# Down projection of the last two token groups: products in eight PSUM banks, raw weights in pieces of 128x512, output DMAs of the group before on another queue

## The chip, the cores and the metric

One Trainium2 chip, of which the kernel uses one core. The metric is the device time of one execution in microseconds; the time given is the median of the runs. The engines are TensorE (PE), VectorE (DVE), ScalarE (ACT), GpSimd (POOL) and SyncE (SP), each with an instruction queue of its own that it works off in order; DMAs are issued from such a queue too.

## What is computed

One layer of a streaming encoder in float32, on 2048 frames of width 1024 with 16 meta tokens ahead of them: RWKV-7 heads and forgetting-attention heads on a common input projection, a common output projection (`w_o`), and a gated MLP with a causal convolution (the Conv-FFN). The change touches the last part alone:

```python
h = x @ w_in                          # 1024 -> 2 x 2816
hp = pad(h, CONV_W - 1 ahead)         # CONV_W = 3
y = conv_b + sum(conv_w[i] * hp[:, i : i + L] for i in range(CONV_W))
u, gt = split(y, 2)
x = x + (silu(gt) * u) @ w_out        # 2816 -> 1024
```

## The kernel before, in words

Every float32 operand of TensorE is split into a high part and a low part in the type `F32R`: ScalarE casts the high part (`h`), VectorE or GpSimd subtracts it from the operand (`l`). A product is three matmuls per 128 of the contracted dimension: high by high, low by high, high by low. All matmuls of these products are issued by one helper, at L1121.

The Conv-FFN works on four groups of some 512 tokens, held with tokens along the free dimension. The hidden dimension is 22 blocks `f` of 128 (`FT`). The first two groups (`early`) go one by one through class `Ffn`: its `down` (L1226 on) multiplies the activated blocks by `w_out` and adds the products to `acc`, the group's residual stream (8 tiles `m` of 128 features by 512 tokens), and after the last block sends each tile to the output. The last two groups, `a` and `b`, go together through class `Last`, after `rest()` has finished the second early group and `w_o` has made their inputs `acca` and `accb`.

`Last` makes the up projection of both groups from seven products in place of eight, as Strassen and Winograd do it: sums of the weights' blocks (`raw` tiles, combined on GpSimd at L1342 to L1353: `s`, and three in place) meet sums of the inputs' blocks (`half_a`, `half_b`: `t1` to `t4`, `b2`, each with `h` and `l`; the `parts` helper is L1267 and L1268, `scaled` is L1273). `up(f)` is a generator for one block: it loads two raw weight tiles of 128x1024 (`ru`, `rg`, L1312), splits them (`qh`, `ql`, `rh`, `rl`: L1322, L1323, L1348, L1349), issues the products into four banks (`A`, `B`, `D`, `Cb`), copies and adds them into four tiles `c`, runs the convolution (`conv`: one ScalarE activation L1338 and two VectorE steps L1340 on a tile `v`), and the activation up to `zh`, `zl` (L1399 to L1405). `mlp` calls it for each `f`, and after every second block the `down` of the pair of blocks before. So there are eleven `down` calls. Each is 16 products of six matmuls: 8 tiles `m` by the groups `a` and `b`, each product in one PSUM bank, then added to `acca` or `accb` by VectorE (L1423). Its weights come in two halves of four `m`; a half is one raw tile of 128x1024, filled by two DMAs of 128x512 (L1414, one for each block of the pair) and split as a whole (L88 on ScalarE, L89 on VectorE).

PSUM has eight banks of 128x512: the pool `ffpA` hands out three (`bank`, name `pp`), the pool `ffpR` five (`bankR`, name `pr`). In the last stage the up projection uses `pr` and the down projection `pp`. SBUF tiles come from pools that are stacked; where a new pool lies on memory of a closed one, its first writes wait for the last uses of what was there. `L0` and `L1` are the pools of the split inputs, `L0` lies first, then `ffV` (`raw`, `qh`/`ql`, `r`, `s1`), then `L1`; they lie where the early groups had `acc`, `xh`, `xl`. `late_ops` lists what goes to `L0`.

The order of instructions on each engine is not written out: the framework schedules the program beforehand against a timeline of its own, which also decides which buffer of a ring an instruction gets. So a change of a ring or a bank moves instructions.

Of the kernel before, what the change touches and what calls it, by code (L numbers as in the profile page):

```python
# [68 lines left out]
def pcol(K, name, i=0):  # L69
    o, w = PC[name]  # L70
    return K.pc[:, o + i : o + i + 1]
# [14 lines left out]
def split(eng, K, src, hi, lo):  # L86

    K.nc.scalar.copy(hi, src)  # L88
    eng.tensor_sub(lo, src, hi.bitcast(F32))  # L89
# [1008 lines left out]
class Ffn:  # L1098
# [128 lines left out]
    def down(self, G, fs, zs):  # L1227
        K, nc, acc = self.K, self.K.nc, G.acc
        w = [self.weight(K.fout[f]) for f in fs]
        for m in range(KC):  # L1230
            ms = slice(128 * m, 128 * m + 128)
            for b, nb in G.blocks:
                p = G.out([128, 512])[:, :nb]
                self.product(p, [(wh[:, ms], wl[:, ms], zh[:, b : b + nb], zl[:, b : b + nb])
                                 for (wh, wl), (zh, zl) in zip(w, zs)])
                a = acc[:, m, b : b + nb]
                nc.vector.tensor_tensor(a, a, p, op=ALU.add)
            if fs[-1] == FT - 1:
                s = max(16 - G.T0, 0)
                nc.sync.dma_start(K.outT[m, :, G.T0 + s - 16 : G.T0 - 16 + G.n], acc[:, m, s : G.n])  # L1240

    def mlp(self, G, switch=FT, out=None):

# [12 lines left out]
class Last:  # L1256
# [51 lines left out]
    def up(self, f):  # L1308
        K, nc, W = self.K, self.K.nc, self.W
# [7 lines left out]
        bank = lambda: self.bank([128, 512])  # L1317
# [15 lines left out]
        vs = {}  # L1333

        def conv(i, j):
            t, k = c[i][j], f + i * FT
            v = vs[i, j] = self.C([128, 512], "v", 3)
            nc.scalar.activation(v, t[:, 2:], AF.Identity, bias=pcol(K, "cb", k), scale=pcol(K, "cw2", k))  # L1338
            for o in (1, 0):
                nc.vector.scalar_tensor_tensor(v, t[:, o : o + 512], pcol(K, f"cw{o}", k), v, op0=ALU.mult, op1=ALU.add)  # L1340
# [5 lines left out]
        for i, v in enumerate((au, ag)):  # L1346
            s = slice(256 * i, 256 * i + 256)
# [60 lines left out]
    def down(self, fs, zs):  # L1408
        K, nc = self.K, self.K.nc
        for m in range(KC):  # L1410
            if m % 4 == 0:
                raw, (h, l) = self.raw(), self.pair()
                for i, f in enumerate(fs):
                    nc.sync.dma_start(raw[:, 512 * i : 512 * i + 512], K.fout[f, :, 128 * m : 128 * m + 512])  # L1414
                split(nc.vector, K, raw, h, l)
                w = [(h[:, s : s + 512], l[:, s : s + 512]) for s in (0, 512)]
            ms = TILES[m % 4]
            for j, G in enumerate((self.a, self.b)):
                t = slice(512 * j, 512 * j + 512)
                p = self.out([128, 512])  # L1420
                self.F.product(p, [(wh[:, ms], wl[:, ms], zh[:, t], zl[:, t]) for (wh, wl), (zh, zl) in zip(w, zs)])
                a = G.acc[:, m]
                nc.vector.tensor_tensor(a, a, p, op=ALU.add)  # L1423
                if fs[-1] == FT - 1:
                    nc.sync.dma_start(K.outT[m, :, G.T0 - 16 : G.T0 - 16 + 512], a)
# [16 lines left out]
def tail(K, ctx, at, c0):  # L1442
# [6 lines left out]
    bank = lambda shape: pA(shape, "pp", 3)  # L1449
    turn = ExitStack()  # L1450
    with ExitStack() as c1:
# [16 lines left out]
        bankR = lambda shape: pR(shape, "pr", 5)  # L1468
# [13 lines left out]
        M = Last(F, a, b)  # L1482
# [2 lines left out]
        F.w_o(b)  # L1485
        rest()

    late_ops = ("t4h", "t4l", "t3h", "t3l", "b2h", "b2l", "rh", "rl")
    L0 = Pool(tc, late, "ffL0", side="left")
    M.W = Pool(tc, late, "ffV", side="left")  # L1490
    L = pools(L0, Pool(tc, late, "ffL1", side="left"), dict.fromkeys(late_ops, 0))
# [6 lines left out]
    turn.close()  # L1498
    M.C = Pool(tc, late, "ffC2", side="left")
    M.Z = Pool(tc, late, "ffZ", side="right")  # L1500
    M.bank, M.out = bankR, bank
    M.mlp()


# [50 lines left out]
```

## Time and profile before

| what | us |
|---|---|
| median of 3 runs | 3417.93 |
| the three runs | 3402.91, 3419.29, 3417.93 |
| the profiled execution | 3404.62 |
| span of the profiled execution | 3402.80 |
| TensorE busy | 3275.4 |
| VectorE busy | 2352.7 |
| ScalarE busy | 1664.9 |
| GpSimd busy | 1159.8 |

The times of the trace run from the span's start; 1.8 us of the profiled execution lie around the span. The last two groups' Conv-FFN takes the span from about 2662 us to the end. `[7.25 <-ACT qh L1322]` behind a row of a timeline means that the engine had idled 7.25 us just before, until ScalarE's instruction of that line had made `qh`. "x12" is the number of instructions that a row joins. The granted clock (PEclk) is a share of TensorE's full speed. An engine's busy time is counted in its instructions; issuing a DMA is not in it.

### The profile page before, as it was taken

To read this page: it belongs to the slowest core of one execution; us is meant where nothing else is said; L and a number is where in the kernel's file an instruction comes from. 1 tells how busy PE (TensorE), PEld (TensorE's weight loads), DVE (VectorE), ACT (ScalarE), POOL (GpSimd) and SP (SyncE) were. 2 spreads that over 40 slices of the span, in tenths; PEclk is the share of its full clock that TensorE was granted. 3 is DMA by queue.
4 is the path that set the end of the run, shared out by engine and by line. 5 is a ranking of instruction groups with operands and counts; after the bars stand their busy time and mean duration, and the time that the engine had idled before them with its cause. 6 is when DMAs were issued, how large, how long until landed. Compare 5 with 4: busy or idle time off the path is not lost.

```text
span 3402.8 us, 61891 instructions
## 1 busy us (share of the span) xinstructions
PE 3275.4 (96%) x23061; PEld 2906.4 (85%) x23061; DVE 2352.7 (69%) x4946; ACT 1664.9 (49%) x3529; POOL 1159.8 (34%) x1733
## 2 busy tenths in 40 slices
PE   7999999999999999999999999999999899999999
PEld 7889888988988988999999998888888677777777
DVE  5665666566556757887878886777665677667666
ACT  5542444554244457765666665654343343334342
POOL 4441112444111157755445453412014422222221
PEclk9999999999999999999999999999999899999999
DMA  4566333356634255333233344324233111111112
GB/s 111 122 133 154 105 93 102 99 121 133 158 88 108 78 172 162 116 107 111 80 89 100 94 130 132 94 73 158 94 98 115 65 50 50 41 53 56 38 50 87
DMA packets 346517, 341.93 MB, mean 100 GB/s; under 512 B 168376, under 2 KB 281256, under 8 KB 345192
## 3 DMA queue, kind: packets, MB, share of 16 engines
q1 hardware_dynamic: 346024, 337.91, 35.1%
q8 instruction: 182, 2.98, 0.4%
q14 instruction: 119, 0.97, 0.1%
q0 software_dynamic: 192, 0.07, 0.0%
HBM read 267.62 MB, written 70.27 MB: 99 GB/s over the span
## 4 chain that ended last, share of the span: by engine, by line
PE 48%; DVE 4%; DMA 3%; ACT 2%; issue 2%; POOL 2%; SPq 0%; ACTq 0%; POOLq 0%; DVEq 0%
PE pp L1121 23%; PE pr L1121 16%; PE o L1031 3%; PE pt L1011 3%; DMA raw<-d_qk 2%; PE s L961 1%; PE s L963 1%; DVE v L1340 1%; DVE rl L1349 1%; DMA raw<-in_fin_dram 1%; POOL kl L903 0%; ACT P L980 0%; ACT ph L1026 0%; DVE ql L89 0%; DVE c L1331 0%
## 5 line engine op out<-in xcount | busy, mean ns | idle before, releaser
L82 DVE TENSOR_TENSOR ww_lo<-ww_raw,ww_hi 128x1024 fp32r<-128x1024 f32 (+1 forms) x172 | 215.5, 1260 | 79.1 <-ACT ww_hi L81 45.0
L1121 PE MATMUL pp<-xh,ww_hi 128*128 128x256 f32 (+2 forms) x1248 | 248.3, 326 | 4.3 <-ACT xh L1186 3.2
L1121 PE MATMUL pp<-xh,ww_lo 128*128 128x256 f32 (+2 forms) x1248 | 250.3, 325 | 0.0
L1121 PE MATMUL pp<-xl,ww_hi 128*128 128x256 f32 (+2 forms) x1248 | 247.9, 324 | 0.0
L81 ACT CAST ww_hi<-ww_raw 128x1024 fp32r<-128x1024 f32 (+1 forms) x172 | 171.4, 1009 | 132.2 <-PE pp L1121 54.9
L1027 DVE TENSOR_TENSOR pl<-pt,ph 128x512 fp32r<-128x512 f32 (+2 forms) x352 | 196.2, 562 | 52.5 <-ACT ph L1026 50.8
L1026 ACT CAST ph<-pt 128x512 fp32r<-128x512 f32 (+2 forms) x352 | 167.6, 485 | 105.1 <-PE pt L1011 73.2
L954 DVE CUSTOM_DVE_ANT_0 P<-cb,s 16x16 f32<-16x16 f32 (+8 forms) x360 | 182.7, 519 | 51.6 <-PE s L963 28.5
L1121 PEld LDWEIGHTS pp<-xh,ww_hi 128*128 128x128 f32 x1248 | 191.2, 189 | 23.9 <-ACT xh L1186 4.5
L1121 PEld LDWEIGHTS pp<-xl,ww_hi 128*128 128x128 f32 x1248 | 194.0, 189 | 17.9
L1121 PEld LDWEIGHTS pp<-xh,ww_lo 128*128 128x128 f32 x1248 | 192.3, 189 | 16.9
L1011 PE MATMUL pt<-cst,P 128*128 128x128 f32 (+2 forms) x1224 | 202.1, 276 | 2.9 <-ACT P L980 1.6
L89 POOL TENSOR_TENSOR wi<-sq,kx 128x320 fp32r<-128x320 f32 (+2 forms) x48 | 48.6, 1012 | 397.7 <-ACT kx L88 296.1
L203 PE MATMUL pj<-xah,w_hi 128*128 128x384 f32 x480 | 166.0, 346 | 1.8 <-ACT xah L194 1.8
L1031 PE MATMUL o<-ph,vs 128*128 128x256 f32 x576 | 158.8, 285 | 6.7 <-ACT ph L1026 6.4
L205 PE MATMUL pj<-xah,w_lo 128*128 128x384 f32 x480 | 164.6, 343 | 0.4 <-DVE r L181 0.4
L204 PE MATMUL pj<-xal,w_hi 128*128 128x384 f32 x480 | 163.6, 341 | 0.0
L1340 DVE SCALAR_TENSOR_TENSOR v<-c,pc,v 128x512 f32<-128x512 f32 x176 | 145.0, 849 | 21.9 <-ACT v L1338 15.3
L1031 PE MATMUL o<-pl,vs 128*128 128x256 f32 x576 | 156.5, 290 | 2.9 <-DVE pl L1027 2.5
L980 ACT ACTIVATE P<-P,nm 128x656 f32<-128x656 f32 (+6 forms) x104 | 143.5, 1380 | 30.7 <-DVE nm L979 30.3
L203 PE MATMUL pj<-xbh,w_hi 128*128 128x320 f32 (+1 forms) x480 | 153.9, 321 | 0.0
L205 PE MATMUL pj<-xbh,w_lo 128*128 128x320 f32 (+1 forms) x480 | 153.8, 320 | 0.0
(501 smaller groups left out, 9859.2 us busy)
## 6 DMA issues: line engine op xcount, KB each, us to landing
ww_raw<-in_fin_dram SPq DMA_DIRECT2D x88, 512.0 KB, 3.6
w_raw<-in_wt_dram SPq DMA_DIRECT2D x60, 512.0 KB, 3.7
ww_raw<-in_fout_dram SPq DMA_DIRECT2D x44, 512.0 KB, 3.7
raw<-in_fin_dram SPq DMA_DIRECT2D x44, 512.0 KB, 3.7
xv<-d_var SPq DMA_DIRECT2D x32, 384.0 KB, 5.9
ww_raw<-in_wo_dram SPq DMA_DIRECT2D x24, 512.0 KB, 3.5
raw<-in_fout_dram SPq DMA_DIRECT2D x44, 256.0 KB, 2.9
raw<-d_qk SPq DMA_DIRECT2D x112, 88.0 KB, 2.6
```

The costliest lines, as they stand in the source:

```text
L81: nc.scalar.copy(hi, raw)
L82: nc.vector.tensor_sub(lo, raw, hi.bitcast(F32))
L203: nc.tensor.matmul(p, wh[:, c, :M], xh[:, c, :n], start=c == 0, stop=False)
L204: nc.tensor.matmul(p, wh[:, c, :M], xl[:, c, :n], start=False, stop=False)
L205: nc.tensor.matmul(p, wl[:, c, :M], xh[:, c, :n], start=False, stop=c == KC - 1)
L954: nc.vector.tensor_tensor_reduce(dst, c, src, 1.0, 3e38, op0=ALU.add, op1=ALU.min, accum_out=mx[:nq, np_ : np_ + 1])
L1011: nc.tensor.transpose(pt[:kn, x, c0 : c0 + nq], P[:nq, k0 : k0 + kn], K.ident[:nq, :nq])
L1026: nc.scalar.copy(ph[:kn, xs, c:N], pt[:kn, xs, c:N])
L1027: nc.vector.tensor_sub(pl[:kn, xs, c:N], pt[:kn, xs, c:N], ph[:kn, xs, c:N].bitcast(F32))
L1031: nc.tensor.matmul(o[:, c:N], vs[:kn, jj], pp[:kn, x, c:N], start=False, stop=jj == nt - 1 and y == 1)
L1121: self.K.nc.tensor.matmul(p, w, x, start=start and i == 0, stop=i == len(mms) - 1, skip_group_check=not start)
L1340: nc.vector.scalar_tensor_tensor(v, t[:, o : o + 512], pcol(K, f"cw{o}", k), v, op0=ALU.mult, op1=ALU.add)
```

## The change

Five edits. (1) In `Ffn.down` the output DMAs of the second early group are issued from GpSimd's queue and no longer from SyncE's. (2) The ring of `v` has two buffers in place of three. (3) In `Last.down` each piece of raw weights, 128x512 for one block of the pair, has a tile `rawd` of its own with one buffer, is loaded by one DMA and split by itself, in place of half a `raw` tile; the split results lie as before in two halves of `qh`, `ql`. (4) `t2l` goes to `L0`, which is then larger by 6 KB in each partition, and `ffV` begins that much further on: `raw` lies no longer on the memory of `acc` but on that of `xh`. (5) The banks for the products of `Last.down` come from `pp` and `pr` in turn; since groups `a` and `b` alternate, `a`'s products are in `pp` and `b`'s in `pr`, which the up projection keeps using.

```diff
--- before.py
+++ after.py
@@ -1,3 +1,4 @@
+import itertools
 import math
 from contextlib import ExitStack
 from types import SimpleNamespace
@@ -1237,7 +1238,8 @@
                 nc.vector.tensor_tensor(a, a, p, op=ALU.add)
             if fs[-1] == FT - 1:
                 s = max(16 - G.T0, 0)
-                nc.sync.dma_start(K.outT[m, :, G.T0 + s - 16 : G.T0 - 16 + G.n], acc[:, m, s : G.n])
+
+                (nc.gpsimd if G.last else nc.sync).dma_start(K.outT[m, :, G.T0 + s - 16 : G.T0 - 16 + G.n], acc[:, m, s : G.n])
 
     def mlp(self, G, switch=FT, out=None):
 
@@ -1334,7 +1336,7 @@
 
         def conv(i, j):
             t, k = c[i][j], f + i * FT
-            v = vs[i, j] = self.C([128, 512], "v", 3)
+            v = vs[i, j] = self.C([128, 512], "v", 2)
             nc.scalar.activation(v, t[:, 2:], AF.Identity, bias=pcol(K, "cb", k), scale=pcol(K, "cw2", k))
             for o in (1, 0):
                 nc.vector.scalar_tensor_tensor(v, t[:, o : o + 512], pcol(K, f"cw{o}", k), v, op0=ALU.mult, op1=ALU.add)
@@ -1409,11 +1411,12 @@
         K, nc = self.K, self.K.nc
         for m in range(KC):
             if m % 4 == 0:
-                raw, (h, l) = self.raw(), self.pair()
-                for i, f in enumerate(fs):
-                    nc.sync.dma_start(raw[:, 512 * i : 512 * i + 512], K.fout[f, :, 128 * m : 128 * m + 512])
-                split(nc.vector, K, raw, h, l)
+                h, l = self.pair()
                 w = [(h[:, s : s + 512], l[:, s : s + 512]) for s in (0, 512)]
+                for f, hl in zip(fs, w):
+                    raw = self.W([128, 512], "rawd")
+                    nc.sync.dma_start(raw, K.fout[f, :, 128 * m : 128 * m + 512])
+                    split(nc.vector, K, raw, *hl)
             ms = TILES[m % 4]
             for j, G in enumerate((self.a, self.b)):
                 t = slice(512 * j, 512 * j + 512)
@@ -1485,7 +1488,7 @@
         F.w_o(b)
         rest()
 
-    late_ops = ("t4h", "t4l", "t3h", "t3l", "b2h", "b2l", "rh", "rl")
+    late_ops = ("t4h", "t4l", "t3h", "t3l", "b2h", "b2l", "rh", "rl", "t2l")
     L0 = Pool(tc, late, "ffL0", side="left")
     M.W = Pool(tc, late, "ffV", side="left")
     L = pools(L0, Pool(tc, late, "ffL1", side="left"), dict.fromkeys(late_ops, 0))
@@ -1498,7 +1501,9 @@
     turn.close()
     M.C = Pool(tc, late, "ffC2", side="left")
     M.Z = Pool(tc, late, "ffZ", side="right")
-    M.bank, M.out = bankR, bank
+    M.bank = bankR
+    banks = itertools.cycle((bank, bankR))
+    M.out = lambda shape: next(banks)(shape)
     M.mlp()
 
 
```

Up to the last output DMAs of the second early group the order on all engines stays as it was; from there on it moves instructions, at these places above all. First GpSimd's queue at the end of `rest()`, where the stage of the last two groups begins (`r` and `E` make the scaling of the last group, `s` and the `raw` rows combine the first raw weights, `rl` is the low part of `rb`). Before:

```order
L1162 TENSOR_TENSOR ssum_32468<-ssum_32468,sqv_32687 128x512 [waits Activation_49]
L1162 TENSOR_TENSOR ssum_32468<-ssum_32468,sqv_32722 128x512 [waits Activation_49]
L1162 TENSOR_TENSOR ssum_32468<-ssum_32468,sqv_32757 128x512 [waits Activation_49]
L1173 TENSOR_TENSOR r_32765<-r_32765,mhalf_76 128x4 [waits DVE_49]
L100 TENSOR_SCALAR E_32769<-r_32765 128x512 [waits Pool_49]
L1342 TENSOR_TENSOR s_6058_32881<-raw_32878 128x384 [waits DMAHW5_49,PE_49]
L1351 TENSOR_TENSOR raw_32878<-raw_32877,raw_32878 128x384 [waits DMAHW3_49,DMAHW2_49,DMAHW4_49,DMAHW1_49,DMAHW6_49,DMAHW0_49,DMAHW7_49,DVE_49,Pool_49]
L1268 TENSOR_TENSOR rl_32938<-xs_6076_32934,rh_32937 128x1024 [waits Activation_49]
```

and now:

```order
L1163 TENSOR_TENSOR ssum_32468<-ssum_32468,sqv_32757 128x512 [waits Activation_49]
L1242 DMA out_dram<-acc_29102 128x512 [waits DVE_49] x5
L1174 TENSOR_TENSOR r_32765<-r_32765,mhalf_76 128x4 [waits DVE_49]
L101 TENSOR_SCALAR E_32769<-r_32765 128x512 [waits Pool_49]
L1242 DMA out_dram<-acc_29102 128x512 [waits DVE_49] x3
L1344 TENSOR_TENSOR s_6058_32881<-raw_32878 128x384 [waits DMAHW5_49,PE_49]
L1353 TENSOR_TENSOR raw_32878<-raw_32877,raw_32878 128x384 [waits DMAHW4_49,Pool_49]
L1354 TENSOR_TENSOR raw_32877<-s_6058_32881,raw_32877 128x384 [waits DVE_49,Pool_49]
L1270 TENSOR_TENSOR rl_32938<-xs_6076_32934,rh_32937 128x1024 [waits DMASW4_49,DMASW3_49,DMASW5_49,DMASW2_49,DMASW6_49,DMASW1_49,DMASW7_49,DMASW0_49,Activation_49]
```

The eight output DMAs stand among these instructions, five ahead of `r` and `E` and three ahead of `s`; `s` now waits for TensorE beside its own DMA.

Second TensorE's queue where a down projection begins, the third (`zh`, `zl` are the activated blocks of the pair, `rh` and `rl` with `pr` the end of the up projection). Before, from the last product of the up projection to the first product that needs a bank again:

```order
L1121 MATMUL pr_34272<-rh_32937,rh_34257 128x512 [waits Activation_49]
L1121 MATMUL pr_34272<-rh_32937,rh_34257 128x512
L1121 MATMUL pr_34272<-rl_32938,rh_34257 128x512 x2
L1121 MATMUL pr_34272<-rh_32937,rl_34258 128x512 x2
L1121 MATMUL pp_34400<-zh_34049,ql_34395 128x512 [waits DVE_49]
L1121 MATMUL pp_34400<-zh_34221,ql_34395 128x512
L1121 MATMUL pp_34408<-zh_34049,ql_34395 128x512
L1121 MATMUL pp_34408<-zh_34221,ql_34395 128x512
L1121 MATMUL pp_34416<-zh_34049,ql_34395 128x512
L1121 MATMUL pp_34416<-zh_34221,ql_34395 128x512
L1121 MATMUL pp_34424<-zh_34049,qh_34394 128x512 [waits DVE_49]
```

and now, from the first row of the down projection on:

```order
L1122 MATMUL pp_34415<-zh_34061,qh_34405 128x512 [waits Activation_49]
L1122 MATMUL pr_34423<-zh_34061,qh_34405 128x512
L1122 MATMUL pp_34431<-zh_34061,qh_34405 128x512
L1122 MATMUL pr_34439<-zh_34061,qh_34405 128x512
L1122 MATMUL pp_34447<-zh_34061,qh_34405 128x512
L1122 MATMUL pr_34284<-rh_32937,rh_34269 128x512 [waits Activation_49]
L1122 MATMUL pr_34284<-rh_32937,rh_34269 128x512
L1122 MATMUL pr_34284<-rl_32938,rh_34269 128x512 x2
L1122 MATMUL pr_34284<-rh_32937,rl_34270 128x512 x2
L1122 MATMUL pr_34455<-zh_34061,qh_34405 128x512 [waits DVE_49]
L1122 MATMUL pr_34471<-zh_34061,qh_34405 128x512 [waits DVE_49]
L1122 MATMUL pp_34415<-zh_34233,qh_34405 128x512 [waits Activation_49]
```

Before, the fourth product (`pp_34424`) waits for VectorE's addition of the first, behind 18 matmuls of three products and six of the up projection. Now the first five products get a bank at once, `pr_34455` and `pr_34471` take banks that the up projection's additions free, and the first row that waits for an addition of this down projection (`pp_34463`) stands 49 matmuls behind the first. The second half's rows that wait for the third and fourth piece of weights stand 48, 56 (casts) and 62, 67 (splits) matmuls behind it, that for the second piece's split 29.

Third VectorE's queue at the same place (`ql` from `raw` or `rawd` are the splits of the down projection's weights, `c` and `v` the convolution of the block, `rl` the next block's weights). Before:

```order
L89 TENSOR_TENSOR ql_34395<-raw_34393,qh_34394 128x1024 [waits DMAHW2_49,DMAHW3_49,PE_49,Activation_49]
L89 TENSOR_TENSOR ql_34466<-raw_34464,qh_34465 128x1024 [waits DMAHW4_49,DMAHW5_49,PE_49,Activation_49]
L1331 TENSOR_TENSOR c_6287_34268<-c_6287_34268,pr_34338 128x512 [waits Activation_49]
L1331 TENSOR_TENSOR c_6286_34267<-c_6286_34267,pr_34307 128x512 [waits PE_49]
L1340 SCALAR_TENSOR_TENSOR v_34537<-c_6287_34268,pc_70,v_34537 128x512 [waits Activation_49]
L1340 SCALAR_TENSOR_TENSOR v_34546<-c_6286_34267,pc_70,v_34546 128x512 [waits Activation_49]
L1340 SCALAR_TENSOR_TENSOR v_34537<-c_6287_34268,pc_70,v_34537 128x512 [waits DVE_49]
L1340 SCALAR_TENSOR_TENSOR v_34546<-c_6286_34267,pc_70,v_34546 128x512 [waits DVE_49]
L1331 TENSOR_TENSOR c_6288_34269<-c_6288_34269,pr_34272 128x512 [waits PE_49]
L1349 TENSOR_TENSOR rl_34572<-raw_34559,rh_34571 128x256 [waits DMAHW6_49,Activation_49]
L1349 TENSOR_TENSOR rl_34572<-raw_34560,rh_34571 128x256 [waits DMAHW7_49,Activation_49]
L1423 TENSOR_TENSOR acca_32134<-acca_32134,pp_34400 128x512 [waits PE_49]
```

and now:

```order
L90 TENSOR_TENSOR ql_34406<-rawd_34407,qh_34405 128x512 [waits DMAHW0_49,PE_49,Activation_49]
L1342 SCALAR_TENSOR_TENSOR v_34340<-c_6289_34278,pc_70,v_34340 128x512 [waits DVE_49]
L1333 TENSOR_TENSOR c_6291_34280<-c_6291_34280,pr_34350 128x512 [waits Activation_49]
L1333 TENSOR_TENSOR c_6290_34279<-c_6290_34279,pr_34319 128x512 [waits PE_49]
L1342 SCALAR_TENSOR_TENSOR v_34555<-c_6291_34280,pc_70,v_34555 128x512 [waits Activation_49]
L90 TENSOR_TENSOR ql_34406<-rawd_34411,qh_34405 128x512 [waits DMAHW5_49,Activation_49]
L1342 SCALAR_TENSOR_TENSOR v_34555<-c_6291_34280,pc_70,v_34555 128x512 [waits DVE_49]
L1333 TENSOR_TENSOR c_6292_34281<-c_6292_34281,pr_34284 128x512 [waits PE_49]
L1351 TENSOR_TENSOR rl_34590<-raw_34577,rh_34589 128x256 [waits DMAHW3_49,Activation_49]
L1351 TENSOR_TENSOR rl_34590<-raw_34578,rh_34589 128x256 [waits DMAHW4_49,Activation_49]
L1402 SCALAR_TENSOR_TENSOR v_34555<-c_6291_34280,v_34555 128x512 [waits Activation_49]
L90 TENSOR_TENSOR ql_34480<-rawd_34481,qh_34479 128x512 [waits DMAHW6_49,Activation_49]
```

The two splits of 1024 columns stood together ahead of additions and convolution steps. Now there are four of 512, one at a time between them; the fourth comes five rows behind the first additions to `acca` and `accb`, which begin two rows below the last row shown.

## Rows read from the trace of the kernel before

**Rows 1.** The page's first part: busy us, share of span, instructions.

```profile
PE 3275.4 (96%) x23061; PEld 2906.4 (85%) x23061; DVE 2352.7 (69%) x4946; ACT 1664.9 (49%) x3529; POOL 1159.8 (34%) x1733
```

**Rows 2.** Windows: busy us by engine, then PEclk, DMA share, GB/s.

```profile
2660.00:2700.00 40.00, 25.07 (x78) 18.22 (x77) 31.60 (x31) 14.85 (x21) 17.95 (x10) 0.74 0.21 73
...
3000.00:3200.00 200.00, 193.50 (x836) 156.32 (x835) 142.20 (x208) 79.16 (x136) 49.59 (x62) 1.00 0.16 50
```

**Rows 3.** What TensorE waited for in 2600:3403: us in total, times, longest us.

```profile
PE pp L1121 <- DVE acca L1423: 20.9, 10, 3.1
...
PE pr L1121 <- ACT t4h L1267: 3.4, 1, 3.4
```

**Rows 4.** TensorE's timeline, a down projection: start us, us, row, [idle before].

```profile
2875.78 0.63 PE L1121 MATMUL pp<-zh,qh 128*128 128x512 f32 x2
...
2879.96 1.56 PE L1121 MATMUL pp<-zh,ql 128*128 128x512 f32 x6
2883.85 0.73 PE L1121 MATMUL pp<-zh,qh 128*128 128x512 f32 x2 [2.32 <-DVE acca L1423]
```

**Rows 5.** VectorE's timeline around the same down projection.

```profile
2873.99 2.46 DVE L89 TENSOR_TENSOR ql<-raw,qh 128x1024 fp32r<-128x1024 f32 x2 [1.28 <-PE pr L1121]
...
2877.93 2.78 DVE L1340 SCALAR_TENSOR_TENSOR v<-c,pc,v 128x512 f32<-128x512 f32 x4 [0.29 <-ACT v L1338]
...
2883.12 0.67 DVE L1423 TENSOR_TENSOR acca<-acca,pp 128x512 f32<-128x512 f32 x1
```

**Rows 6.** Groups of instructions in 2700:3403: VectorE's splits and its 128x512 operations.

```profile
L1402 DVE SCALAR_TENSOR_TENSOR v<-v,v 128x512 f32<-128x512 f32 x44 | 30.0, 683 | 0.0
...
L89 DVE TENSOR_TENSOR ql<-raw,qh 128x1024 fp32r<-128x1024 f32 x22 | 26.3, 1224 | 14.6 <-PE pr L1121 12.2 <-ACT qh L88 2.4
```

**Rows 7.** SyncE's queue where the last two groups begin.

```profile
2651.72 10.93 SPq L1240 DMA_DIRECT2D out_dram<-acc  x8
2664.94 0.82 SPq L1312 DMA_DIRECT2D raw<-in_fin_dram  x2
```

**Rows 8.** TensorE's timeline where the last two groups begin.

```profile
2661.40 0.60 PE L103 MATMUL pp<-cst,E 128*128 128x128 f32 x4
2669.25 5.49 PE L1121 MATMUL pr<-p,qh 128*128 128x512 f32 x12 [7.25 <-ACT qh L1322]
...
2690.82 1.65 PE L1121 MATMUL pr<-t2h,qh 128*128 128x512 f32 x3 [0.75 <-ACT c L1361]
```

**Rows 9.** GpSimd's timeline where the last two groups begin.

```profile
2658.04 1.02 POOL L1173 TENSOR_TENSOR r<-r,mhalf 128x4 f32<-128x4 f32 x1 [5.63 <-DVE r L1172]
...
2670.04 6.67 POOL L1342 TENSOR_TENSOR s<-raw 128x384 f32<-128x384 f32 x1 [10.28 <-DMA raw<-in_fin_dram]
```

**Rows 10.** VectorE's timeline where the last two groups begin.

```profile
2656.55 0.69 DVE L1237 TENSOR_TENSOR acc<-acc,pr 128x512 f32<-128x512 f32 x1 [0.70 <-PE pr L1121]
...
2669.14 1.75 DVE L1268 TENSOR_TENSOR b2l<-b,b2h 128x1536 fp32r<-128x1536 f32 x1
2670.81 1.02 DVE L1323 TENSOR_TENSOR ql<-raw,qh 128x384 fp32r<-128x384 f32 x2
...
2677.29 0.92 DVE L1323 TENSOR_TENSOR ql<-s,qh 128x384 fp32r<-128x384 f32 x1 [1.46 <-ACT qh L1322]
2678.66 3.40 DVE L1268 TENSOR_TENSOR t1l<-xs,t1h 128x1536 fp32r<-128x1536 f32 x1 [0.46 <-ACT t1h L1267]
2681.99 2.55 DVE L1294 TENSOR_TENSOR xs<-xs,t 128x1536 f32<-128x1536 f32 x1
2684.46 2.29 DVE L1323 TENSOR_TENSOR ql<-raw,qh 128x384 fp32r<-128x384 f32 x3
```

**Rows 11.** DMA issues: KB each, median us from issue to landing.

```profile
raw<-in_fout_dram SPq DMA_DIRECT2D x44, 256.0 KB, 2.9
...
out_dram<-acc SPq DMA_DIRECT2D x16, 256.0 KB, 2.5
```

**Rows 12.** The DMAs that GpSimd issues before the change: ns min/median/max.

```profile
L282 POOL DMA_DIRECT2D d_fl<-st x6: 520/647/785, 49.9 to 671.1; - x6
```

## The prediction

> **What bounds the kernel now.** I read the page's first part, then the window table of the last stage, TensorE's waits in it, and the timelines of the engines that these waits name. TensorE is busy 96% of the span [rows 1], so a gain can only come from its idle time, or from fewer matmuls, and the change leaves their number as it is. In the Conv-FFN of the last two token groups one stretch of 200 us holds 193.5 us of matmuls, while VectorE, the next busiest, has 142 us of work in it [rows 2]: it is not a bound on the mean, but it may be late at a place. The list of waits says where: in ten of the eleven down projections a matmul waits for the first addition into `acca`, 20.9 us in all [rows 3]. The other large piece is the stretch in which the last two groups begin: 25.07 of 40 us busy, 14.9 us idle, at a mean granted clock of 0.74 [rows 2].
>
> In a down projection TensorE starts at 2875.78, fills the three `pp` banks with products, works them off to the low parts, and then needs a bank that VectorE has read; it idles 2.32 us and goes on at 2883.85 [rows 4]. VectorE comes late because it has two splits of 1024 columns (2.46 us), four convolution steps (2.78) and smaller work ahead of that addition, which starts at 2883.12 [rows 5]. That is a shortage of banks for a moment, not of VectorE's time.
>
> At the start of the last two groups, SyncE issues eight output DMAs from 2651.72 on, for 10.93 us, each behind an addition, and the first raw weights of the new stage only behind them, at 2664.94 [rows 7]: their buffer lies where `acc` lies. TensorE is done with the old stage at 2662.0, starts the new one at 2669.25 after 7.25 us of waiting for the cast of these weights, and reaches 2690.82 through further waits [rows 8], 3.4 us of them for `t4h` [rows 3].
>
> **The change, part by part.**
>
> *Banks.* The order shows that group a's products keep the three `pp` banks and group b's go to the five `pr` banks. Before, the product that waits stands behind 24 matmuls, 18 of three products and six of the up projection. Now the first row that waits for an addition of this down projection has 49 matmuls ahead of it (48 and one for the other ring). At 193.5/836 = 0.231 us a matmul [rows 2] that is 11.3 us after the start, where the first addition ends 2883.12 + 0.67 - 2875.78 = 8.0 us after it [rows 4, 5]. It may come 3.3 us later than now before TensorE waits. So I take the whole 20.9 us as gone. Bounds: all of it, or none, should another wait stand in its place (rivals).
>
> *Raw weights in pieces.* Twenty-two splits of 1024 columns become 44 of 512 on VectorE and as many casts on ScalarE. On VectorE two operations of 512 columns cost 2 x 0.683 against 1.224 us [rows 6], 0.14 us more, 3.1 us over 22. They are hidden by VectorE's 58 us of idle time in 200 [rows 2]; with that cover gone the price would be those 3.1 us. ScalarE is busy 79 us in 200 [rows 2], so its part is nothing. The DMAs stay 44 of 256 KB. But there is one buffer, so the four pieces of a down projection follow one another: a piece is loaded when the one before is split, and a link is 2.9 us from issue to landing [rows 11], about 0.7 for the cast and 0.68 for the split [rows 6], some 4.3 us (an estimate from these rows, the cast taken like the split). The order shows when TensorE needs the second, third and fourth piece split: behind 29, 48 (its cast) and 67 matmuls, so 6.7, 11.1 and 15.5 us after the start. Three links of 4.3 are 12.9 us behind the split of the first, which VectorE makes before the start. Behind a waiting split stand convolution steps and the additions that free banks, and they have the 3.3 us above. Taken: 0; bounds 0 and the price of the slower rival.
>
> *Two `v` buffers instead of three.* The convolution steps of a block follow one another more tightly. What they make (`z`) is used a block later, so I take 0; what it can cost is VectorE's first addition coming late, and that has the same 3.3 us.
>
> *The start of the last two groups.* With `t2l` moved, the raw weights lie behind `acc`. Their first load waits for TensorE's last reading of `xh`, before the first output DMA of 2651.72, and the eight output DMAs leave SyncE's queue for GpSimd's. The weights took at most 2670.04 - 2664.94 = 5.1 us to come [rows 7, 9], so now they are there by 2657, and their casts can be done before TensorE asks at 2662.0. GpSimd's `s` stands behind the last output DMA (2662.65 at SyncE, [rows 7]); even at its 6.67 us [rows 9] it ends near 2669.7, not 2676.7. But TensorE does not gain the 7.25 us, for the next steps hang on VectorE's queue: up to 2669.14 it is as before, and it then has the same list in another order [rows 10]. In it were, before, 1.46 and 0.46 us of idle time waiting for casts of the late weights; `t1l` took 3.40 and `xs` 2.55, where the same shape takes 1.75 in the first of these rows; and three `ql` took 2.29, where two take 1.02 (0.51 each). Idle 1.92, stretching 1.65 + 0.80 + 0.76 = 3.21, together 5.1 us, all while GpSimd worked on the late weights. I take these 5.1 us as the gain. Bounds: nothing, or the whole 14.9 us of idle time.
>
> The output DMAs cost GpSimd issuing time that SyncE used to spend. Its six small ones before took 0.52 to 0.79 us each [rows 12]. Five of the new ones stand ahead of `r` and `E`, on which the scaling waits; the additions that release them come 0.69 + 0.70 = 1.39 us apart [rows 10], so at 0.65 us the queue is empty when `r` may start at 2658.04 [rows 9]. The cast `b2h` (ScalarE) and the split `b2l` (VectorE), and what is queued behind, wait for all eight to land: 2662.65 + 0.65 + 2.5 [rows 7, 11, 12] is 2665.8, ahead of 2669.14. Taken: 0; the upper bound is a rival.
>
> *The end.* Its last addition is still followed by one DMA on SyncE: 0.
>
> **Sum**, against the profiled execution of 3404.62 us: 3404.6 - 20.9 - 5.1 = 3378.6. That execution lies 13.3 us under the median of the three runs shown, 3417.93; of the four times two lie near 3403 and two near 3418, so I add half of the 13.3, which gives 3385 us.
>
> **The rivals.** All times carry the same 6.7 us.
> 1. *Half the wait comes back.* With two `v` buffers VectorE comes to the first addition more than 3.3 us later than now, and some 1 us per pair stays. For it: VectorE had 1 to 3 us of lateness at this place; against it: 58 us idle in 200. 3404.6 - 5.1 - 10.5 + 6.7 = 3396.
> 2. *The wait only changes its name.* TensorE no longer waits for `acca`, but two us per pair for a piece's split or a `pr` bank of the next up projection. The change would then not do what it says in the steady state: 3404.6 - 5.1 + 6.7 = 3406.
> 3. *Output DMAs clog GpSimd.* At 3.3 us each, half of the 6.67 that `s` took while VectorE was busy [rows 9], five take 16.5 us where there are 6.3 between 2651.72 and 2658.04 [rows 7, 9]: `E` is 10.2 us late, and so is all that follows. The point from which it costs is 1.39 us per DMA. The 5.1 us still come off: 3404.6 - 20.9 + 10.2 - 5.1 + 6.7 = 3396; without them, should the three DMAs ahead of `s` hold it up too, 3401, which I take. Against it: the six small ones [rows 12].
>    The Trainium skill has a rule for this (SBUF — State Buffer, the box on the "DVE blocks DMA" trap): a DMA issued from GpSimd has its descriptors written by GpSimd's cores, which a VectorE operation in a two-port mode locks out, and it gives about 3.1 us instead of 0.62 for such a DMA. By its figure the rival would come out at about the same time. The same page limits this to two-port modes and says a two-input operation only meets GpSimd's reads, and no run here shows an output DMA from GpSimd yet; so it has a small chance.
> 4. *Slower: the chain of pieces is the bound.* If each link waits 2.5 us more on VectorE, ScalarE or SyncE (a pair of convolution steps takes half of 2.78 [rows 5]; loads of the next up projection share the queue), three links are 7.5 us late, against 15.5 - 12.9 = 2.6 of reserve: 4.9 us in each of eleven down projections, 54 us, less the 20.9 that go, 33 more: 3404.6 - 5.1 + 33 + 6.7 = 3439. It begins to cost at 0.9 us per link, and eats the gain at about 1.6. For it: one buffer instead of two, and in-order queues. Against: the order puts a split between single convolution steps, not behind four.
>
> **How the numbers follow.** Chances: forecast 0.52, rival 1 0.15, rival 2 0.12, rival 3 0.08, rival 4 0.13. The range goes from 3364 (all 14.9 us of the start gone too, and runs like the profiled one) to 3412 (rival 2 and a little more); it leaves out rival 4 and some of the edges. A measurement of this kernel can tell about 0.5% from no change, 17 us: faster is under 3401. That takes 0.47 from the forecast, 0.10 from rival 1 and 0.05 from 2 and 3, 0.62; the same 0.25; slower is rival 4, 0.13.
>
> **What would show it.** Right: no wait for `acca` over 1 us before the last down projection; about 98% busy in 3000:3200, with no other wait in its place; the first `raw` loads landing before 2660 and TensorE's `t2h` product near 2685.7. Wrong: waits of TensorE for `ql`, `qh` or a `pr` bank in each pair (rivals 1, 2, 4), `E` later than 2662 or output DMAs over 1.4 us on GpSimd (rival 3).

## The result, and the profile after

| | before | changed kernel |
|---|---|---|
| median of 4 runs | 3418.61 us (3402.91 to 3423.53) | 3379.0 us (3376.43 to 3390.31) |
| ratio of the runs | | 0.9898, 95% interval 0.9859 to 0.9937 |
| profiled execution | 3404.62 us | 3390.31 us |
| span | 3402.80 us | 3388.5 us |

The changed kernel is about 1% faster. The two medians lie 39.6 us apart, the two profiled executions 14.3 us. Neither number is the change's own: the order of all engines is the same up to the end of the early groups, yet that place comes at another time in each execution. So I cut each span there. A is the end of the last matmul of the early group (a row `pr<-zh,ww_lo`, start plus duration), B the start of the first `t2h` product, both from TensorE's timeline. What an edit does, at the start or behind it, stands in the columns behind A.

| kernel | A | A to B | B to the end of the span | A to the end |
|---|---|---|---|---|
| before | 2661.56 | 29.26 | 711.98 | 741.24 |
| changed | 2669.98 | 27.49 | 691.03 | 718.52 |

By this cut the change takes 22.7 us out: 1.8 at the start of the last two groups and 20.9 behind it. Spans, by contrast, differ by 8.4 us before the change begins: 2669.98 against 2661.56.

The windows of the changed kernel (columns as in [rows 2]; the PEclk is the third number from the end):

```profile
2660.00:2700.00 40.00, 24.36 (x94) 18.43 (x93) 31.99 (x36) 13.45 (x17) 24.42 (x19) 0.86 0.25 93
...
3000.00:3200.00 200.00, 200.00 (x867) 162.55 (x866) 147.32 (x228) 82.12 (x147) 56.74 (x67) 1.00 0.17 52
3200.00:3340.00 140.00, 139.11 (x602) 112.67 (x602) 102.92 (x158) 59.92 (x108) 38.76 (x45) 1.00 0.14 42
3340.00:3389.00 49.00, 42.48 (x179) 32.80 (x177) 28.94 (x45) 7.03 (x11) 2.58 (x2) 0.99 0.35 117
```

Between 3000 and 3200 TensorE is busy without a gap, 867 matmuls where [rows 2] had 836. What TensorE waits for in 2600:3403 now:

```profile
PE pr L1122 <- ACT t4h L1269: 6.8, 1, 6.8
PE pr L1122 <- DVE ql L1325: 5.0, 1, 5.0
PE pr L1122 <- DVE t1l L1270: 3.0, 1, 3.0
PE pp L1122 <- ACT qh L89: 2.0, 2, 1.1
PE pp L1122 <- ACT zh L1406: 1.0, 1, 1.0
...
PE pp L1122 <- DVE acca L1426: 0.7, 2, 0.4
```

The 20.9 us for `acca` [rows 3] are 0.7. New are two waits for the cast of a piece of weights (L89) and one for `zh`. At the start the wait for the first cast, 7.25 us [rows 8], has gone, and three others have grown in its place. TensorE's timeline there:

```profile
2669.82 0.60 PE L104 MATMUL pp<-cst,E 128*128 128x128 f32 x4
2670.18 3.04 PE L1122 MATMUL pr<-p,qh 128*128 128x512 f32 x12
2678.17 2.88 PE L1122 MATMUL pr<-p,ql 128*128 128x512 f32 x6 [4.95 <-DVE ql L1325]
...
2686.45 0.96 PE L1122 MATMUL pr<-t1l,qh 128*128 128x512 f32 x3 [2.98 <-DVE t1l L1270]
...
2694.96 1.65 PE L1122 MATMUL pr<-t4h,qh 128*128 128x512 f32 x3 [6.85 <-ACT t4h L1269]
2697.47 1.65 PE L1122 MATMUL pr<-t2h,qh 128*128 128x512 f32 x3 [0.86 <-ACT c L1363]
```

The weights are in time, and the first twelve matmuls follow `E` at once, in 3.04 us against 5.49. The cause of the long wait for `t4h` stands in GpSimd's timeline:

```profile
2665.95 0.54 POOL L1242 DMA_DIRECT2D out_dram<-acc  x1 [0.85 <-DVE acc L1238]
...
2671.56 1.04 POOL L1344 TENSOR_TENSOR s<-raw 128x384 f32<-128x384 f32 x1
2672.68 1.01 POOL L1353 TENSOR_TENSOR raw<-raw,raw 128x384 f32<-128x384 f32 x1
2678.26 9.95 POOL L1354 TENSOR_TENSOR raw<-s,raw 128x384 f32<-128x384 f32 x1 [4.57 <-DVE ql L1325]
```

An output DMA costs GpSimd 0.54 us. `s` takes 1.04 where it took 6.67 [rows 9], but now a later subtraction of the same size takes 9.95, while VectorE works through its operations of 128x1536; ScalarE's next cast waits for it, and the casts for `t2h`, `t3h` and `t4h` stand behind that cast:

```profile
2688.24 0.51 ACT L1324 CAST qh<-raw 128x384 fp32r<-128x384 f32 x1 [8.26 <-POOL raw L1354]
...
2693.43 1.47 ACT L1269 CAST t4h<-xs 128x1536 fp32r<-128x1536 f32 x1 [1.94 <-DVE xs L1296]
```

The last of them waits 1.94 us more for `xs`, which stands in VectorE's queue behind the split of the same `qh` (L1325, 2.15 us from 2688.78).

### The profile page after: what moved, and what is told of

Read it like the earlier page. It is cut to its first block, busy times and chain, and to the rows that moved or that the text cites. A ratio compares the mean times of both kernels' runs of the same rounds, so it can differ in the third digit from the quotient of the medians.

```text
span 3388.5 us, 61944 instructions
## 1 busy us (share of the span) xinstructions
PE 3275.3 (97%) x23061; PEld 2907.6 (86%) x23061; DVE 2345.6 (69%) x4968; ACT 1671.2 (49%) x3551; POOL 1177.0 (35%) x1741
## 4 chain that ended last, share of the span: by engine, by line
PE 47%; DVE 4%; DMA 3%; POOL 2%; issue 2%; ACT 2%; SPq 0%; POOLq 0%; ACTq 0%; DVEq 0%
PE pr L1122 20%; PE pp L1122 19%; PE o L1032 2%; PE pt L1012 2%; DMA raw<-d_qk 2%; PE s L962 1%; PE s L964 1%; POOL kl L904 1%; DVE v L1342 1%; DMA rawd<-in_fout_dram 0%; DVE pl L1028 0%; ACT P L981 0%; DVE ww_lo L83 0%; DVE P L955 0%; POOL kq L907 0%
```

## The experiments

All are cut at A and B like the two above. The question was which of the five edits gives what.

| kernel | A | A to B | B to end | A to end |
|---|---|---|---|---|
| e1: before, banks in turn | 2670.43 | 29.24 | 684.63 | 713.87 |
| e2: changed, three banks | 2666.60 | 27.48 | 732.72 | 760.20 |
| e4: changed, `t2l` back | 2672.70 | 29.12 | 689.18 | 718.30 |
| e5: changed, shared raw ring | 2664.80 | 25.45 | 685.65 | 711.10 |
| e3: changed, output DMAs on SyncE | 2670.27 | 29.26 | 690.57 | 719.83 |
| e6: changed, three `v` | 2675.27 | 27.48 | 687.25 | 714.73 |
| e7: changed, combinations on VectorE | 2670.66 | 24.01 | 689.83 | 713.84 |
| e9: banks, `t2l`, DMAs on GpSimd | 2674.22 | 25.45 | 683.03 | 708.48 |
| e12: e9, combinations on VectorE, `E` first | 2672.66 | 22.23 | 683.11 | 705.34 |
| e11: e9, `E` first | 2663.46 | 25.12 | 684.22 | 709.34 |
| e13: changed, two pieces | 2661.50 | 27.49 | 686.31 | 713.80 |

Each edit was profiled once. Between A and B that is enough: the changed kernel, e2, e6 and e13, which differ only in the down projections and the convolution, take 27.48 or 27.49 us there. Behind B up to 2 us are TensorE's clock and not the edit: over the first 20 us behind B the granted clock is 0.88 in the changed kernel, 0.90 in e1 and e5, and 1.00 in e9, and a tenth of 20 us is 2 us.

**e1: the banks alone.**

```diff
-    M.bank, M.out = bankR, bank
+    M.bank = bankR
+    banks = itertools.cycle((bank, bankR))
+    M.out = lambda shape: next(banks)(shape)
```

> The kernel before with one edit: the banks of the last down projections' products come from the three and the five in turn. Theory (the wait for acca is a shortage of banks alone): TensorE's 20.9 us of waits for acca go, from the t2h product of the new stage to the end of the span it takes about 691 us like the changed kernel (712.0 before), and the start of the stage stays as before, 29.4 us from the matmuls of E to t2h. Rival (the pieces of weights or the two v buffers are needed for it, since two splits of 1024 columns hold VectorE): 5 to 20 us of waits for acca or ql stay, 696 to 711 us.

Measured: 684.63 us from B to the end, 27.4 less than before and 6.4 less than the changed kernel; below what either theory gave. TensorE's list of waits from 5 us before `E` to the end is five rows, all of them at the start of the stage, nearly as in the kernel before:

```profile
PE pr L1122 <- ACT qh L1323: 7.5, 1, 7.5
PE pr L1122 <- ACT t4h L1268: 3.4, 1, 3.4
PE pr L1122 <- DVE t1l L1269: 2.0, 1, 2.0
PE pr L1122 <- ACT t1h L1268: 1.7, 1, 1.7
PE pr L1122 <- ACT c L1362: 0.7, 1, 0.7
```

So the wait was a shortage of banks alone, and two splits of 1024 columns did no harm. It also shows that the stalls cost more than their idle time: 21.4 us of waits behind B went (`acca`, `accb`, `zl`), and the stretch is 27.4 shorter. Part of the rest is TensorE's clock. Around the longest stall of the kernel before, of 3.09 us, the granted clock over 2816:2822 was 0.72, and its matmuls ran apart by some 0.43 us in place of 0.23 until 2821.7:

```profile
2817.27 0.73 PE L1121 MATMUL pp<-zh,qh 128*128 128x512 f32 x2 [3.09 <-DVE acca L1423]
2817.84 0.70 PE L1121 MATMUL pp<-zl,qh 128*128 128x512 f32 x2
2818.34 1.05 PE L1121 MATMUL pp<-zh,ql 128*128 128x512 f32 x2
2819.19 1.05 PE L1121 MATMUL pp<-zh,qh 128*128 128x512 f32 x2
```

```profile
2816.00:2822.00 6.00, 4.73 (x14) 3.72 (x15) 4.29 (x8) 1.34 (x2) 1.80 (x3) 0.72 0.00 0
```

In those 6 us 14 matmuls ran where e1 has 28; the 1.27 us of idle time in them explain 5 or 6 of the 14 missing, and the lower of TensorE's two clock levels (1.2 in place of 2.4 GHz) some 7: at 0.72 it takes 0.28 x 6 = 1.7 us. Another part is that the listed idle time begins where the last matmul ends. In [rows 4] six matmuls start from 2879.96 on, so at 0.231 us each the next could start at 2881.35; it starts at 2883.85, 2.50 us later, where 2.32 are listed. Over ten stalls that is some 2 us. What is left of the 6.0 us between 21.4 and 27.4, some 2 us, is not accounted for.

**e2: the changed kernel without the banks.**

```diff
-    M.out = lambda shape: next(banks)(shape)
+    M.out = bank
```

> The changed kernel with the last down projections' products back in three banks. Theory: the waits for acca are back, 15 to 21 us, 706 to 712 us from t2h to the end; the start of the stage like the changed kernel, 27.7 us. Rival (spreading the splits between VectorE's other work is what took the wait away): under 8 us of waits, 691 to 699 us.

Measured: 732.72 us, 20.7 more than the kernel before and outside both. The waits for `acca` are back as the theory had it, and waits for the pieces come on top:

```profile
PE pp L1122 <- DVE acca L1426: 21.2, 12, 2.8
PE pp L1122 <- ACT qh L89: 7.1, 9, 2.4
```

With three small ones the waits behind B are 29.9 us, where the kernel before had 21.4, so 8.5 of the 20.7 us are idle time. About half is TensorE's clock. In e2 seven stalls have a stretch of 6 us around or behind them with a granted clock of 0.72, like this one:

```profile
3286.00:3292.00 6.00, 5.15 (x15) 4.11 (x16) 5.54 (x10) 2.67 (x4) 1.29 (x1) 0.72 0.32 87
```

In the kernel before it is one of ten (the one shown under e1). Six more, at 1.7 us each, are some 10 us. The spreading of the splits, then, took nothing away; with three banks the pieces and the two `v` buffers cost. That is slower, as rival 4 of the prediction has it, but not by its sum: it put 4.9 us on each down projection, and TensorE waits 2.42 us for a piece in the first, 0.40 in seven of the middle ones and 1.92 in the tenth.

**e5, e6 and e13: what costs the 6.4 us between e1 and the changed kernel.** In e5 `Last.down` is as before (the shared ring `raw`, splits of 1024 columns). In e6 and e13:

```diff
-            v = vs[i, j] = self.C([128, 512], "v", 2)
+            v = vs[i, j] = self.C([128, 512], "v", 3)
```

```diff
-                    raw = self.W([128, 512], "rawd")
+                    raw = self.W([128, 512], "rawd", 2)
```

> The changed kernel with the down projections' raw weights back in the shared ring of two 128x1024 tiles. Theory (banks alone do it): no wait for acca over 1 us before the last down projection, 691 to 693 us from t2h to the end. Rival (the pieces matter in the steady state): 3 to 15 us of new waits for acca, ql or for the next block's weights that share the ring, 694 to 706 us. At the start the order has the splits and the first products ahead of E's matmuls here, so the scaling begins some 8 us later on TensorE: the time from the last acc product to t2h is 27 to 31 us by both.

> The changed kernel with three v buffers again, the pieces of weights kept. From t2h to the end the changed kernel takes 691.0 us, 6.4 more than the banks alone (684.6). Theory (the pieces through one buffer cost it): 690 to 692 us again, with the same waits of TensorE for qh and zh. Rival (the two v buffers cost it): 684 to 687.

> The changed kernel with two buffers for the pieces of raw weights in place of one. Theory (what the pieces cost beside the two v buffers, 5.4 us from t2h to the end against the shared ring, is the chain of loads: with one buffer a piece comes every 4.1 to 4.3 us, and the last two down projections need eight in a row): 685 to 687.5 us from t2h to the end (691.0 with one buffer, 685.7 with the shared ring), TensorE's waits for the casts of the pieces under 0.5 us in all (2.0). Rival (the order around smaller splits costs it, not the loads): 689.5 to 692.

Measured: e5 came out under what was expected at both places, 685.65 and 25.45 us, with no wait for `acca`. The two `v` buffers alone (e5 against e1) cost 1.0 us, the pieces alone (e6 against e1) 2.6, both 6.4. The reference is e1 although it lacks the edits at the start: e9, which has them, takes 683.03 us, 1.6 less than e1, but with the higher clock behind B that the table's note gives. In e6 neither of the two theories held: TensorE waits 0.2 us for a piece in place of 2.0, and 687.25 lies just above the rival's range, for each edit makes the other dearer. With a second buffer for the pieces (e13) 4.7 of it are gone, as the theory there had it, and TensorE waits for no piece. ScalarE's casts of the pieces in the last two down projections of the changed kernel show the chain:

```profile
3352.84 0.62 ACT L89 CAST qh<-rawd 128x512 fp32r<-128x512 f32 x1 [4.40 <-DMA rawd<-in_fout_dram]
3357.15 0.62 ACT L89 CAST qh<-rawd 128x512 fp32r<-128x512 f32 x1 [3.69 <-DMA rawd<-in_fout_dram]
3361.28 0.62 ACT L89 CAST qh<-rawd 128x512 fp32r<-128x512 f32 x1 [3.51 <-DMA rawd<-in_fout_dram]
3361.80 0.61 ACT L1406 CAST zh<-v 128x512 fp32r<-128x512 f32 x1
```

Here a piece comes every 4.1 to 4.3 us, each cast waiting for its DMA; the longest link of these eight, from 3337.22 to 3343.48, took 6.3. In the middle of the loop that is soon enough, as the stretch of 3000 to 3200 shows. The last two down projections follow one another and need eight pieces; there, and in the first, TensorE waits, as its timeline tells:

```profile
2755.30 0.49 PE L1122 MATMUL pp<-zh,qh 128*128 128x512 f32 x1 [1.10 <-ACT qh L89]
...
3337.89 0.50 PE L1122 MATMUL pp<-zh,qh 128*128 128x512 f32 x1 [0.89 <-ACT qh L89]
...
3362.47 0.50 PE L1122 MATMUL pp<-zh,qh 128*128 128x512 f32 x1 [1.02 <-ACT zh L1406]
```

What is different there is how far ahead the chain begins. In the eight down projections between, the second piece is cast 2.0 us behind the down projection's first matmul (3003.93 against 3001.96); in the first it is 3.9 (2754.62 against 2750.69), in the tenth 3.2 (3337.22 against 3334.07). The product that waits stands 13 matmuls behind the first one, some 3.0 us at 0.231 us each. The `zh` of the last wait is cast at 3361.80, right behind a piece's cast that had itself waited 3.51 us. With the shared ring the start is also shorter (25.45 us in e5 and e9): there the scheduler put the first block's splits between the additions into `acc`, and 24 matmuls of the new stage ahead of those of `E` (in e5 from 2664.64 to 2670.23). That difference is there before the kernel runs; why a tile of 2 KB makes the scheduler choose so is not settled.

**e4 and e3: the start of the stage, undone from either side.**

```diff
-    late_ops = ("t4h", "t4l", "t3h", "t3l", "b2h", "b2l", "rh", "rl", "t2l")
+    late_ops = ("t4h", "t4l", "t3h", "t3l", "b2h", "b2l", "rh", "rl")
```

```diff
-                (nc.gpsimd if G.last else nc.sync).dma_start(K.outT[m, :, G.T0 + s - 16 : G.T0 - 16 + G.n], acc[:, m, s : G.n])
+                nc.sync.dma_start(K.outT[m, :, G.T0 + s - 16 : G.T0 - 16 + G.n], acc[:, m, s : G.n])
```

> The changed kernel with t2l back in the second pool, so that the first raw weights lie again on the memory of acc. Theory (what the start gained comes from the weights being early): first raw loads behind all eight output DMAs, 29 to 31 us from the matmuls of E to t2h (27.7 in the changed kernel, 29.4 before); 691 us from t2h to the end. Rival (it comes from the output DMAs having left SyncE's queue): 27.7 us stay.

> The changed kernel with the output DMAs of the group before back on SyncE's queue; in the order the first raw loads then stand behind six of the eight. Theory (what the start gained comes from the raw weights being early, and for that both the memory and the queue have to be free): 28 to 29.5 us from the last acc product to the t2h product (27.5 in the changed kernel, 29.3 before), 691 us from t2h to the end. Rival (the move of t2l alone does it): 27 to 27.7.

Measured: 29.12 and 29.26 us from A to B, so either undoes the whole gain; the rivals fall, and memory and queue both have to be free. In e3 SyncE's queue shows the loads behind seven output DMAs:

```profile
2660.43 9.54 SPq L1242 DMA_DIRECT2D out_dram<-acc  x7
2670.07 0.87 SPq L1314 DMA_DIRECT2D raw<-in_fin_dram  x2
```

B to the end, 689.2 and 690.6 us, was as expected for the changed kernel within 2 us.

**e7: why the start gave 1.8 us and not more.**

```diff
+        eng = nc.gpsimd if f else nc.vector
-        nc.gpsimd.tensor_sub(a21, a11, a21)
-        nc.gpsimd.tensor_sub(a11, s1, a11)
-        nc.gpsimd.tensor_sub(a12, a12, a11)
+        eng.tensor_sub(a21, a11, a21)
+        eng.tensor_sub(a11, s1, a11)
+        eng.tensor_sub(a12, a12, a11)
```

> The changed kernel, but the three in-place combinations of the first block's raw weights run on VectorE and not on GpSimd. Theory (the start of the stage gained 1.8 us and not 5.1 because one of them, 1.0 us of work, took 9.95 us on GpSimd beside VectorE's additions of two SBUF inputs, and the cast for t4h stood behind it): 24 to 25 us from the last acc product to t2h (27.5), TensorE's wait for t4h under 4 us (6.8). Rival (VectorE's own queue sets it, and three operations more there make it longer): 27.5 to 29. 691 us from t2h to the end by both.

Measured: 24.01 us, 3.5 less, and 1.2 us of waiting for `t4h` in place of 6.8. The theory holds: the start was held by GpSimd's subtraction of 9.95 us. GpSimd is slowed still, where it no longer matters; its `rl` (128x1024, 2.69 us in the kernel before) now lies alone beside VectorE's chain:

```profile
2672.23 1.03 POOL L1344 TENSOR_TENSOR s<-raw 128x384 f32<-128x384 f32 x1
2677.86 20.93 POOL L1270 TENSOR_TENSOR rl<-xs,rh 128x1024 fp32r<-128x1024 f32 x1 [4.60 <-ACT rh L1269]
```

**e9, e11, e12: a version that beats both.** e9 is the kernel before with three of the five edits: banks, `t2l`, and output DMAs on GpSimd. e11 and e12 put the matmuls of `E` ahead of the new stage's products; e12 has the edit of e7 too.

```diff
-        nc.tensor.transpose(o, e[:, i], K.ident[:m, :m])
+        K.spread = nc.tensor.transpose(o, e[:, i], K.ident[:m, :m]).ins
...
-        mm(A, w1, self.p1)
+        if f:
+            mm(A, w1, self.p1)
+        else:
+            with K.tc.issue_after(K.spread):
+                mm(A, w1, self.p1)
```

> The kernel before with three of the five edits: the banks in turn, t2l in the first pool, the output DMAs on GpSimd; three v buffers and the shared raw ring stay. Theory: 684 to 685.5 us from t2h to the end (banks alone 684.6, with two v buffers 685.7), and 25 to 26 us from the last acc product to t2h, as with the raw ring and two v buffers (25.5), since the order there is the same: 709 to 711 us in all, where the changed kernel has 718.5 and the kernel before 741.2. Rival (the gain of the start there came from the two v buffers): 27.5 to 29.3 us to t2h.

> The kernel of the banks in turn, t2l in the first pool, output DMAs on GpSimd, three v buffers and the shared raw ring, with two more edits at the start of the last two groups: the first block's in-place combinations on VectorE, and the first product of the new stage ordered behind the matmuls of E. Theory (there TensorE waits for VectorE's chain that begins with E's matmuls, and 29 to 34 products of the new stage stand ahead of them in the queue without need): E's matmuls within 1.5 us of the last acc product, 20.5 to 23 us from that product to t2h (25.5 without the two edits), 683 to 685 us from t2h to the end, 704 to 708 in all; against the kernel before some 1.0% faster, 0.985 to 0.992. Rival (GpSimd's rl, 16 to 21 us beside VectorE's additions, is the next to be waited for once the rest is earlier): 24 to 27 us to t2h, or a wait for rl of several us behind it.

> As e12_best, but the first block's combinations stay on GpSimd, three of them ahead of E there. Theory: E comes some 3 us later than in e12_best, 23 to 25 us from the last acc product to t2h. Rival (E is not delayed by them): the same as e12_best within 0.7 us.

Measured: e9 708.48 us from A to the end, just under what was expected; behind B it is 683.03, with TensorE's clock up from B on. e12 705.34, as expected: 13.2 less than the changed kernel and 35.9 less than the kernel before, each by its own profile. Timed against the kernel before, e12 is 3374.49 us (4 runs) against 3414.26 (7 runs), ratio 0.9884, interval 0.9861 to 0.9906. In e11, with the combinations still on GpSimd ahead of `E`, TensorE waits 3.8 us for `E`, in e12 1.2:

```profile
2673.88 0.66 PE L104 MATMUL pp<-cst,E 128*128 128x128 f32 x4 [1.22 <-POOL E L101]
...
2683.16 1.37 PE L1122 MATMUL pr<-t1h,qh 128*128 128x512 f32 x3 [3.02 <-ACT t1h L1268]
2689.27 1.65 PE L1122 MATMUL pr<-t1l,qh 128*128 128x512 f32 x3 [4.74 <-DVE t1l L1269]
```

e11 is 0.1 us above its range, so being first in TensorE's queue gains little unless `E` is early too. What remains in e12 are waits for VectorE's own chain, with no idle time in it.

## Why the prediction was right, and where its terms were off

The time, 3379.0 us, lies in the range and near the forecast of 3385, and the gain is beyond what a measurement can tell from no change. The sum made it 26.0 us against the profiled execution; cut at A it was 22.7, in other parts than the sum had them.

- *Banks, 20.9 us.* Right in mechanism: the 49 matmuls ahead of the first row that waits for an addition were cover enough, and the wait is gone. Mis-sized: alone they give 27.4 us (e1). The prediction counted the idle time in the list of waits and left out what a stall costs beside it: 2.50 us of delay in the same rows where 2.32 are listed, and at the longest stall a stretch at the lower clock.
- *Pieces, taken at 0, and two `v` buffers, taken at 0.* This is the step that failed: together they give back 6.4 us (e1 against the changed kernel). The link of some 4.3 us was right (4.1 to 4.3 in most, 6.3 in the longest), and in the middle of the loop nothing waits. But the step took the second piece as needed at its split, 29 matmuls behind the start, and the row of the order that needs its cast first, `pp_34415<-zh_34233,qh_34405`, stands 13 behind it, 3.0 us. In the middle that cast comes 2.0 us behind the start; in the first and the tenth down projection it comes 3.9 and 3.2 us behind, and TensorE waits 1.10 and 0.89. In the eleventh, right behind the tenth, no up projection hides the chain. The rest of the "banks" term paid for it, so that the sum behind B came out at 20.9 by accident.
- *The start, 5.1 us.* 1.8 measured. The weights came early as forecast, and `s` was quick. But the estimate took all of GpSimd's slow work for a result of the late weights. It moved to another subtraction of the same set, 9.95 us, and cost there 3.5 us (e7). The idle time of 4.95 us for `ql` was foreseen in kind: VectorE had the splits behind the scaling, but no term of the sum held it.
- *Output DMAs on GpSimd, 0.* Right: 0.54 to 0.69 us each, under the 1.39 between the additions; `r` and `E` were not late. Rival 3 falls. The Trainium skill's rule on DMAs from GpSimd (SBUF — State Buffer, section "SBUF: two separate sides", the box on the "DVE blocks DMA" trap) did not bite here: it is about two-port modes, and the additions beside these DMAs, `acc<-acc,pr`, have one input in SBUF. From issue to landing the eight took a median of 3.0 us, where the eight that SyncE still issues for the first early group took 3.2 in the same run.
- *Rivals 1 and 2.* No wait per pair came back in the changed kernel. Rival 4 did not decide; its late pieces show at 1 us in the first and the tenth down projection of the changed kernel, and in e2, where they are a part of the 20.7 us.
- *The median.* The 6.7 us added for the spread of the runs were a guess at the right thing with the wrong size: the place A alone lies between 2661.50 and 2675.27 us in thirteen profiles whose order of instructions is the same until at least some 10 us ahead of it, and the profiled execution of the kernel before is among the earliest. So it is luck that 3379.0 came within 6 us of 3385: 22.7 us off the median before would be 3395.9, inside the range too. The three other executions of the changed kernel took 10.0 to 13.9 us less than the profiled one, at a mean granted clock of 0.985 to 0.987 where that one had 0.984.

## What to carry to other kernels

Price a buffer that is made smaller at the ends of its loop, where the work that hides its loads is missing, and not in the middle alone. Where executions differ by more than the change, cut the profiles at a place ahead of which nothing changed, compare what lies behind it, and read the granted clock on both sides of the cut. An edit that comes in a bundle should be tried alone: here one of the five gave 27.4 us where all five gave 22.7, and three of them with two new ones gave 35.9.

## What was not expected of the hardware

A short GpSimd operation can take many times as long beside VectorE's operations with two SBUF inputs: 128x384 took 1.0 us beside operations with one input in PSUM and 9.95 beside those, 128x1024 took 2.69 where VectorE's queue had a gap and 20.93 where it had none. That agrees with what the Trainium skill says (SBUF — State Buffer, section "Who interferes with whom"): a VectorE operation with two SBUF inputs and a GpSimd operation that reads SBUF keep each other out. What the runs add is the scale of it where VectorE's queue has no gap: in e7 `rl` starts at 2677.86 and ends at 2698.79, 2.2 us behind the last of that chain (`t4l`, until 2696.55), and in the changed kernel the 9.95 us end at 2688.21, in a gap of 1.45 us on VectorE.

In the kernel before, the granted clock was 0.72 over 2816:2822, around a stall of 3.09 us, and 1.00 over 2884:2888, behind one of 2.32 [rows 4]. So of two stalls that differ by 0.8 us one had no stretch at the lower clock behind it, and the other lost some 1.7 us more to one. In e2 seven stalls did, two of them behind idle times of 2.24 and 2.29 us, while one of 2.43 us (2889:2895, granted clock 1.00) did not: the length of the stall does not decide it alone.

The part ahead of A differs by up to 13.8 us between executions with the same order, and the granted clock goes with it. Over the first 1000 us of the span it is 0.98 in the four profiles with the earliest A (2661.50 to 2664.80), 0.97 in the changed kernel (2669.98) and 0.96 in e6 (2675.27), and a hundredth of 1000 us is 10 us; over 200:300 it is 0.97 in e13, which has the earliest A, and 0.91 in e6. Why executions of one order get a different clock was not tried.
